# A decoder layer on one core: when x by tokens is loaded, where one block of x by features stands among the first weights, and which queue reloads the decay products

## The chip, the core and the metric

The kernel runs on one core of a Trainium2 chip. The core has TensorE (PE, matmuls), VectorE (DVE), ScalarE (ACT) and GpSimd (POOL) for arithmetic, and SyncE (SP), which here only issues transfers. SP, ACT and POOL each issue transfers from their own instruction stream, in order; a transfer that must wait for something holds up everything behind it on that engine. All transfers share 16 DMA engines. The metric is device time in microseconds (us) of one execution, lower is better.

## What is computed

One decoder layer, float32, 256 tokens by 2048 features, batch 1. Cut to the order of its parts:

```
def reference(x, mem, ...):
    x = x + 0.5 * swiglu(rms_norm(x, ffn1_norm), ffn1_w_gate, ffn1_w_up, ffn1_w_down)   # d_ff 5632
    x = gated_parallel_mixer(x, ...)      # p = rms_norm(x) @ w_in; sliding-window attention beside
                                          # RWKV-7 time mixing; gated sum @ w_out
    x = memory_cross_attention(x, mem, ...)
    x = x + 0.5 * swiglu(rms_norm(x, ffn2_norm), ffn2_w_gate, ffn2_w_up, ffn2_w_down)
    return rms_norm(x, final_norm)

def swiglu(h, w_gate, w_up, w_down):
    return (silu(h @ w_gate) * (h @ w_up)) @ w_down
```

RWKV-7 is a recurrence over time with a removal term. The kernel computes it in chunks of 128 tokens, which needs the inverse of a triangular matrix of products of decayed keys for each head and chunk. Those are the "decay products" of the change.

## The kernel before

**Weights.** All weights are read from DRAM once, in an order written out in `weight_plan` (L105) and cut into items of two 128-row blocks (L260 to L268). `load` (L275) issues an item's transfer on SP; in the feed-forward stages one unpaired load brings two items (1 MB, `wide`, L290), and a paired item (gate and up, or two column blocks of down) takes two transfers of 512 KB (L285). In the feed-forward stages there are three buffers of 1 MB (`raw2`, `RAW = 3`); in the mixer, four of 512 KB. A load waits on SP until its buffer is free.

**Products.** For precision every float32 operand is split in two: `hi`, its value cast to the matmul's format on ACT (L308), and `lo`, the rest, by a subtraction on DVE (L309). A product is three matmuls, hi by hi, lo by hi and hi by lo (`times`, L393: L396, L397, L398). `product` (L374) goes through the items of a column block; `next_item` (L356) issues loads ahead, splits the item and up to two items more, and returns the parts. `product_pair` (L454) is the paired form, in which some items take seven block products in place of eight: for these, `sums` (L321) makes differences of raw weights on DVE (L328 to L330) and splits them (L333, L334).

**Background work.** Everything else (norms, attention, the recurrence) is written as generators, which `Interleave` (L60) steps once in each tick; `product` ticks after each token half of an item, `product_pair` some 29 times in a column block. `idle(n)` (L175) lets n ticks pass. This sets the order in which the instructions are written down. From it the framework fixes the order on each engine when the program is built; on the chip an engine runs its instructions in that order, each as soon as what it needs is there. An instruction that waits for nothing runs as soon as its engine comes to it, however late its tick.

**The start (L762 to L790).** x by features (`xT`, for the matmuls' stationary side) is loaded in four blocks of 512 KB into `turned[0..3]`, the first in two halves, interleaved by hand on SP with the first loads of the gate weights:

```
first half of block 0, load 0 (one piece on ACT, two on SP), second half of block 0,
load 2 (two halves), block 1, load 4, block 2, load 6, block 3, load 8
```

`Norm.features` (L636) scales a block on ACT (`xhi`, L642) and takes the rest on DVE (`xlo`, L643); `squares` (L653) squares it on ACT (L655) and adds it up on DVE (L658, L662) for 1/rms, which reaches the first silu (L717) by PE (L667), DVE (L679) and POOL (L681). x by tokens, to which the results of the feed-forward are added, is loaded by `residual` (L785): four blocks of 512 KB over POOL's queue, 24 ticks apart. Its first reader is the end of the first down product (L570).

**The decay products (L1026 to L1114).** `removal_keys` computes them on PE and DVE and stores them over POOL to `ld` in DRAM (L1088), four times. `substitute` (L1093) reloads the diagonal blocks of 32 x 32 as `dl` with four transfers on SP (L1098), runs of 128 bytes, then waits 14 ticks and does the forward substitution in 62 small steps on DVE (L1105, L1110).

## Time and profile before

| | us |
|---|---|
| median of 3 runs (2276.04 to 2277.23) | 2276.31 |
| the profiled execution | 2275.04 |
| its span, first to last instruction | 2273.3 |
| PE busy in the span | 2248.3 |
| DVE busy | 1742.7 |
| ACT busy | 1213.6 |
| POOL busy | 128.9 |

The mean granted clock of PE over the span was 0.998. The DMA engines moved 434.63 MB, 191 GB/s on average.

How the views are read. A row of a timeline has start, duration, engine, line, operation, and written tile <- read tiles; the square brackets give the idle time ahead of it and what ended it. A row of the windows has the stretch, its length, then busy time and number of instructions of PE, PEld (weight loads of PE), DVE, ACT and POOL, the granted PE clock (1.00 is full), the mean busy share of the DMA engines and GB/s. A row of waits has who waited, for what, the sum, how many times, and the longest. A row of DMA issues has the tiles, the queue (SPq, POOLq), the number of transfers, KB each and the median us from issue to landing. The matmuls' durations overlap, since they are pipelined; in a full stretch one starts every 0.2275 us or so.

### The profile page before, as it was taken

Reading aid. Unit: us, or ns where it says so; the run is one execution under the profiler, and the core shown is the slowest. Engines: PE = TensorE matmul, PEld = TensorE weight load, DVE = VectorE, ACT = ScalarE, POOL = GpSimd, SP = SyncE. Lnnn points to the kernel's source line nnn. Section 1 sums busy time; section 2 is a strip of 40 time slices with the busy share of each in tenths; the row PEclk is TensorE's granted clock in tenths of the full one; section 3 lists DMA queues with packets and bytes.
Section 4 is the critical chain, followed back from the end, with each engine's and each line's share of the span. In section 5 each row is a group of like instructions: output and inputs, shape, how many; then the busy total and the mean of one; then the engine's idle time right before and its main releaser. Section 6 shows DMA issues by size and latency. Waiting matters only on the chain.

```text
span 2273.3 us, 28304 instructions
## 1 busy us (share of the span) xinstructions
PE 2248.3 (99%) x10588; PEld 1842.6 (81%) x10588; DVE 1742.7 (77%) x2120; ACT 1213.6 (53%) x1611; POOL 128.9 (6%) x184
## 2 busy tenths in 40 slices
PE   8999999999999999999999999999999999999998
PEld 6888888888888777788888888888888887888886
DVE  6988988889887567795444566547898888898887
ACT  6555555555555576444344546456555455555554
POOL 1000000000000001101220020001000000000002
PEclk9999999999999999999999999999999999999999
DMA  7665665666566545766432576557655665566664
GB/s 261 203 201 188 204 204 189 200 198 197 198 200 202 151 138 158 222 214 203 117 107 88 163 265 231 192 165 256 203 192 189 209 199 193 188 200 204 199 201 156
DMA packets 222890, 434.63 MB, mean 191 GB/s; under 512 B 17840, under 2 KB 19968, under 8 KB 222752
## 3 DMA queue, kind: packets, MB, share of 16 engines
q1 hardware_dynamic: 213840, 404.80, 55.8%
q0 software_dynamic: 8336, 27.22, 3.7%
q8 instruction: 83, 1.36, 0.2%
q10 hardware_dynamic: 576, 0.79, 0.1%
q14 instruction: 55, 0.45, 0.1%
HBM read 419.65 MB, written 13.11 MB: 190 GB/s over the span
## 4 chain that ended last, share of the span: by engine, by line
PE 93%; DVE 3%; DMA 2%; issue 1%; ACT 1%; POOL 0%; SPq 0%; POOLq 0%; ACTq 0%; DVEq 0%
PE acc L396 19%; PE acc L397 19%; PE acc L398 19%; PE mm L397 8%; PE mm L398 8%; PE mm L396 8%; PE tr L593 2%; PE tr L397 2%; PE tr L398 1%; PE tr L396 1%; PE mm L1247 1%; DVE lo L309 1%; PE tr L1216 1%; DMA raw<-in_ffn_w_gate_dram 1%; DMA raw<-in_ffn_w_up_dram 1%
## 5 line engine op out<-in xcount | busy, mean ns | idle before, releaser
L308 ACT CAST hi<-raw 128x1024 fp32r<-128x1024 f32 (+1 forms) x770 | 763.7, 1000 | 792.8 <-PE acc L398 393.9
L309 DVE TENSOR_TENSOR lo<-raw,hi 128x1024 fp32r<-128x1024 f32 (+1 forms) x770 | 891.2, 1168 | 373.7 <-ACT hi L308 372.5
L396 PE MATMUL acc<-hi,xhi 128*128 128x512 f32 (+1 forms) x1196 | 476.8, 399 | 7.7 <-ACT xhi L642 4.6
L397 PE MATMUL acc<-lo,xhi 128*128 128x512 f32 (+1 forms) x1196 | 466.0, 390 | 2.0 <-DVE lo L309 2.0
L398 PE MATMUL acc<-hi,xlo 128*128 128x512 f32 (+1 forms) x1196 | 464.9, 389 | 0.0
L396 PEld LDWEIGHTS acc<-hi,xhi 128*128 128x128 f32 x1196 | 224.9, 188 | 58.0 <-ACT xhi L642 5.5
L397 PEld LDWEIGHTS acc<-lo,xhi 128*128 128x128 f32 x1196 | 225.4, 188 | 48.2 <-DVE lo L309 3.2
L398 PEld LDWEIGHTS acc<-hi,xlo 128*128 128x128 f32 x1196 | 225.0, 188 | 47.0 <-issue 0.6
L333 ACT CAST thi<-raw 128x1024 fp32r<-128x1024 f32 x160 | 166.0, 1052 | 73.9 <-DVE raw L328 36.5
L334 DVE TENSOR_TENSOR tlo<-raw,thi 128x1024 fp32r<-128x1024 f32 x160 | 192.8, 1218 | 1.3 <-ACT thi L333 1.3
L397 PE MATMUL acc<-lo,hhi 128*128 128x512 f32 x404 | 158.0, 391 | 0.0
L398 PE MATMUL acc<-hi,hlo 128*128 128x512 f32 x404 | 157.8, 391 | 0.0
L396 PE MATMUL acc<-hi,hhi 128*128 128x512 f32 x404 | 157.3, 392 | 0.0
L396 PE MATMUL mm<-hi,xhi 128*128 128x512 f32 x380 | 149.1, 392 | 0.0
L397 PE MATMUL mm<-lo,xhi 128*128 128x512 f32 x380 | 148.3, 390 | 0.0
L398 PE MATMUL mm<-hi,xlo 128*128 128x512 f32 x380 | 148.1, 390 | 0.0
L328 DVE TENSOR_TENSOR raw<-raw 128x1024 f32<-128x1024 f32 x80 | 97.5, 1219 | 24.4 <-DMA raw<-in_ffn_w_up_dram 22.6
L397 PEld LDWEIGHTS acc<-lo,hhi 128*128 128x128 f32 x404 | 75.9, 188 | 17.4 <-DVE lo L309 2.3
L396 PEld LDWEIGHTS acc<-hi,hhi 128*128 128x128 f32 x404 | 75.9, 188 | 16.1 <-DVE x L551 0.9
L398 PEld LDWEIGHTS acc<-hi,hlo 128*128 128x128 f32 x404 | 75.9, 188 | 15.4
L397 PEld LDWEIGHTS mm<-lo,xhi 128*128 128x128 f32 x380 | 71.4, 188 | 15.6 <-DVE lo L309 0.6
L398 PEld LDWEIGHTS mm<-hi,xlo 128*128 128x128 f32 x380 | 71.3, 188 | 14.7
(374 smaller groups left out, 3407.4 us busy)
## 6 DMA issues: line engine op xcount, KB each, us to landing
raw<-in_ffn_w_gate_dram SPq DMA_DIRECT2D x167, 512.0 KB, 3.8
raw<-in_ffn_w_up_dram SPq DMA_DIRECT2D x160, 512.0 KB, 4.7
raw<-in_ffn_w_down_dram SPq DMA_DIRECT2D x152, 512.0 KB, 4.8
raw<-in_w_in_dram SPq DMA_DIRECT2D x136, 512.0 KB, 3.7
raw<-in_w_out_dram SPq DMA_DIRECT2D x32, 512.0 KB, 4.6
raw<-in_ffn_w_down_dram SPq DMA_DIRECT2D x12, 1024.0 KB, 5.2
raw<-in_ffn_w_up_dram SPq DMA_DIRECT2D x8, 1024.0 KB, 7.0
raw<-in_w_proj_attn_dram SPq DMA_DIRECT2D x16, 512.0 KB, 3.7
```

The lines of the kernel that those rows point to most:

```text
L308: newest["act"] = act.copy(hi[:, s], raw[:, s])
L309: newest["dve"] = dve.tensor_tensor(lo[:, s], raw[:, s], f32(hi[:, s]), ALU.subtract)
L328: dve.tensor_tensor(ta[:], raw[:, 1:3], raw[:, 0:2], ALU.subtract)
L333: act.copy(hi[:, s], t[:])
L334: dve.tensor_tensor(lo[:, s], t[:], f32(hi[:, s]), ALU.subtract)
L396: pe.matmul(o, xh, hi, start=first, stop=False, **how)
L397: pe.matmul(o, xh, lo, start=False, stop=False, **how)
L398: pe.matmul(o, xl, hi, start=False, stop=last, **how)
L593: pe.transpose(b[:, o : o + P], tok[:, t, col : col + P], ident[:])
L1216: pe.matmul(b[e][:, m * P : (m + 1) * P], x1[r, j, cs_], x2[r, j, cs_], start=True, stop=True,)
L1247: pe.matmul(vb[:, o : o + P][:, r], lhs(e), rhs[:, r], start=first and e == 0, stop=True, **ek,)
```

## The change

Three edits.

1. x by tokens is no longer loaded over POOL. `residual` waits 40 ticks, then 20 ahead of each block, and issues the block on SP, ordered behind the newest paired weight load (`newest["load"]`, which `load` now notes).
2. Among the first loads, block 1 of x by features goes ahead of the second half of load 2 (a piece of `load` may now be a call, `j is None`); blocks 2 and 3 then stand on both sides of load 4; loads 6 and 8 are left to `next_item`. The order on SP becomes: first half of block 0, load 0, second half of block 0, first half of load 2, block 1, second half of load 2, block 2, load 4, block 3, load 6, load 8.
3. The four reloads of the decay products are issued by POOL and not by SP.

```diff
@@ in load @@
             for v, c, to in zip(w, c0, (raw[:, 0:4:3], raw[:, 1:3])):
-                nc.sync.dma_start(
+                newest["load"] = nc.sync.dma_start(
                     to, v[rows, c : c + 512].rearrange("(a p) n -> p a n", p=P)
                 )
...
         for j, queue in pieces or ((slice(0, m * KU), nc.sync),):
+            if j is None:
+                queue()
+                continue
@@ the start @@
-        load(2, ((slice(0, 2), nc.sync), (slice(2, 4), nc.sync)))
-        for n in range(1, 4):
+        load(2, (
+            (slice(0, 2), nc.sync),
+            (None, lambda: nc.sync.dma_start(turned[1], a["xT"][:, 4:8])),
+            (slice(2, 4), nc.sync),
+        ))
+        for n in range(2, 4):
             nc.sync.dma_start(turned[n], a["xT"][:, 4 * n : 4 * n + 4])
-            load(2 * n + 2)
+            if n < 3:
+                load(2 * n)
...
         def residual():
+            yield from idle(40)
             for n in range(4):
-                yield from idle(24)
-                pool.dma_start(col(n), blk(W["x"], n))
+                yield from idle(20)
+                with tc.issue_after(newest["load"].ins):
+                    nc.sync.dma_start(col(n), blk(W["x"], n))
@@ in substitute @@
-                nc.sync.dma_start(dl[q], ld[q, :, q].rearrange("t h s -> h t s"))
+                pool.dma_start(dl[q], ld[q, :, q].rearrange("t h s -> h t s"))
```

## The prediction, made before the changed kernel was seen

> **What bounds the kernel now.** First the page: the busy line and the shares of the chain that ended last.

> ```profile
> PE 2248.3 (99%) x10588; PEld 1842.6 (81%) x10588; DVE 1742.7 (77%) x2120; ACT 1213.6 (53%) x1611; POOL 128.9 (6%) x184
> ...
> PE 93%; DVE 3%; DMA 2%; issue 1%; ACT 1%; POOL 0%; SPq 0%; POOLq 0%; ACTq 0%; DVEq 0%
> ```

> TensorE (PE) is busy for 2248.3 of 2273.3 us. The change removes no matmul, so all it can win is inside the other 25.0 us, or in stretches where PE is busy at a lower clock. Next I cut the span into windows of 20 us and looked for those where PE is not busy throughout. The six largest (columns: length, then busy us and count of PE, PEld, DVE, ACT, POOL; clock; DMA share; GB/s):

> ```profile
> 0.00:20.00 20.00, 14.80 (x67) 12.14 (x68) 9.89 (x18) 11.02 (x17) 8.59 (x34) 1.00 0.91 312
> 20.00:40.00 20.00, 17.11 (x70) 13.19 (x68) 15.00 (x20) 13.74 (x18) 1.48 (x1) 0.91 0.89 310
> 40.00:60.00 20.00, 19.13 (x84) 15.88 (x85) 15.69 (x25) 11.66 (x14) 0.09 (x1) 1.00 0.52 167
> 960.00:980.00 20.00, 18.15 (x80) 14.70 (x80) 17.80 (x44) 7.38 (x7) 0.72 (x1) 1.00 0.69 231
> 1900.00:1920.00 20.00, 18.28 (x81) 14.79 (x80) 18.11 (x21) 11.43 (x14) 0.00 (x0) 1.00 0.61 190
> 2260.00:2273.30 13.30, 4.97 (x22) 3.77 (x21) 4.30 (x10) 4.12 (x8) 1.13 (x2) 0.76 0.42 158
> ```

> The start loses 5.20 + 2.89 + 0.87 = 8.96 us, the end 8.33, and one window in the middle, 960 to 980, loses 1.85. The change touches the start (loads of x and of the first weights) and the reload of the decay products, which lies just before 960. It touches nothing at 1900 or at the end. So I read those two places.

> The start, by the stretches between PE's stops, and PE's first instruction after each stop:

> ```profile
> 12.84:15.31 2.47, 0.00 (x0) 0.00 (x0) 1.24 (x2) 1.09 (x3) 0.00 (x0) 1.00 1.03 392
> 15.31:20.87 5.56, 5.56 (x24) 4.43 (x24) 3.05 (x7) 2.21 (x4) 0.00 (x0) 1.00 1.04 389
> 20.87:23.19 2.32, 0.18 (x1) 0.00 (x1) 0.59 (x1) 1.60 (x3) 0.00 (x0) 1.00 1.02 389
> 23.19:28.60 5.41, 5.22 (x15) 3.89 (x16) 5.41 (x8) 5.17 (x9) 0.00 (x0) 0.68 1.05 391
> ```
> ```profile
> 15.31 0.50 PE L396 MATMUL acc<-hi,xhi 128*128 128x512 f32 x1 [2.47 <-ACT xhi L642]
> ...
> 23.19 0.50 PE L396 MATMUL acc<-hi,xhi 128*128 128x512 f32 x1 [2.14 <-ACT xhi L642]
> 23.88 0.50 PE L397 MATMUL acc<-lo,xhi 128*128 128x512 f32 x1 [0.18 <-DVE lo L309]
> ...
> 40.87 0.50 PE L396 MATMUL acc<-hi,xhi 128*128 128x512 f32 x1 [1.43 <-ACT hb L717]
> ```

> The DMA engines are full (share 1.02 to 1.05, 389 to 392 GB/s) while PE waits. What ScalarE (ACT) was waiting for:

> ```profile
> 9.73 1.05 ACT L308 CAST hi<-raw 128x1024 fp32r<-128x1024 f32 x1 [0.46 <-DMA raw<-in_ffn_w_gate_dram]
> ...
> 12.32 1.05 ACT L308 CAST hi<-raw 128x1024 fp32r<-128x1024 f32 x1 [0.58 <-DMA raw<-in_ffn_w_gate_dram]
> 14.75 1.71 ACT L642 ACTIVATE xhi<-xt,g_first 128x256 fp32r<-128x256 f32 x4 [1.38 <-DMA xt<-in_xT_dram]
> ...
> 21.52 1.04 ACT L308 CAST hi<-raw 128x1024 fp32r<-128x1024 f32 x1 [3.45 <-DMA raw<-in_ffn_w_gate_dram]
> ```

> Both large stops end with a transfer: the second block of x by features (14.75) and the third load of weights (21.52). Who fills the DMA engines is in the list of issues:

> ```profile
> x<-in_x_dram POOLq DMA_DIRECT2D x4, 512.0 KB, 10.5
> ...
> xt<-in_xT_dram SPq DMA_DIRECT2D x3, 512.0 KB, 16.5
> ```
> ```profile
> L788 POOL DMA_DIRECT2D x<-in_x_dram x4: 712/727/733, 6.5 to 8.6; - x4
> L570 DVE TENSOR_TENSOR x<-hb,x x4: 1216/1218/1218, 221.9 to 262.2; 128x1024 f32<-128x1024 f32 x4
> ```

> x by tokens (4 x 512 KB, 2.10 MB) is issued at 6.5 to 8.6 us, since GpSimd (POOL) has nothing to wait for and `idle(24)` delays only its place in the program. Its first reader runs at 221.9. It takes 2.10 MB / 390 GB/s = 5.4 us of a DMA system that PE is waiting for.

> **The change, part by part.** *x by tokens.* On SyncE's queue (SP) it sits behind paired weight loads that wait for free buffers, so it leaves the start. From about 9 to 21 us the weight queue then has the whole rate. The first half of load 2 lands at 9.73, as now; from there one 512 KB piece takes 524 KB / 390 = 1.35 us. In the new order: second block of x at 11.1, second half of load 2 at 12.4, third block of x at 13.8, load 4 (1 MB) at 16.5, fourth block at 17.8, load 6 at 20.5. Before, the second block came at 14.75 and load 4 at 21.52.

> *The block ahead of half a weight.* If the four scalings `xhi` go as the block lands, ACT does them in 11.1 to 12.8 (1.71 us, the row at 14.75), and PE, done with its first 24 matmuls at 12.84, goes on at once; the second half lands at 12.4, is cast after them (1.05) by 13.9, its rest is needed at 12.84 + 2.73 = 15.57 (12 matmuls, half of the 24 that would take 24 x 0.2275 = 5.46; the stretch of 5.56 shows it). If ACT keeps the old order (cast first), the scalings start at 12.4 + 1.05 = 13.45 and PE at about 13.9, 1.1 late. ACT's order is fixed when the program is built and follows readiness as the framework supposes it; a block ahead in the queue speaks for the first, which I take. Load 4 at 16.5 gives its cast by 17.6 and its rest by 18.8; PE needs them at 18.3 (cast) and 18.5 (rest). So stops of 2.47, 2.32 and 0.18 go. So does the low clock behind the second: 5.41 us at 0.68 lose 5.41 x 0.32 = 1.73 us. Sum: 6.70.

> What is late next is VectorE (DVE), whose work for a block of x and its two weight pieces is

> ```profile
> 15.29 1.69 DVE L643 SCALAR_TENSOR_TENSOR xlo<-xt,g_first,xhi 128x256 fp32r<-128x256 f32 x4 [0.67 <-ACT xhi L642]
> ...
> 18.11 1.23 DVE L658 TENSOR_TENSOR xt<-xt 128x1024 f32<-128x1024 f32 x1 [0.97 <-ACT xt L655]
> ```

> 1.69 + 1.23 + two rests of 1.22 (the `lo` row below) = 5.36 us against PE's 5.46. No cushion, so I give back 0.5 in small waits (bounds 0 and 1.1, the old order above). The wait of 1.43 at 40.87 ends with a chain of squares and 1/rms; PE arrives 6.7 us sooner, the DVE part of the chain perhaps not as much: another 0.5 (bounds 0 and 1.5). Start: 6.70 - 1.0 = 5.7 us won.

> *x behind the weights, between 90 and 170 us.* The program place is 60, 80, 100 and 120 ticks; a paired column block is about 29 ticks, the first two products about 36. Each issue costs SP under half a microsecond, each transfer 1.35 us behind a load, so it can make only the next load late. The closest the trace shows there:

> ```profile
> 70.00:170.00 100.00, 100.00 (x446) 81.92 (x445) 90.64 (x105) 57.45 (x64) 0.00 (x0) 1.00 0.60 196
> ```
> ```profile
> 92.80 1.23 DVE L328 TENSOR_TENSOR raw<-raw 128x1024 f32<-128x1024 f32 x1 [2.49 <-DMA raw<-in_ffn_w_up_dram]
> ...
> 100.90 1.23 DVE L334 TENSOR_TENSOR tlo<-raw,thi 128x1024 fp32r<-128x1024 f32 x1
> ```
> ```profile
> 104.91 0.39 PE L396 MATMUL tr<-thi,chi 128*128 128x512 f32 x1
> ```

> Even where DVE sat 2.49 us for a late load, the last difference made from it was done at 102.13 and PE read it at 104.91: 2.8 us of cover over 1.35. DMA is at 0.60 there. I cost it at 0; with the cover gone it is up to 4 x 1.35 = 5.4.

> *Decay products over GpSimd.* Now SP holds this (waits of SP's queue, then its issues):

> ```profile
> SPq L1098 <- DMA ld<-lt: 4.0, 1, 4.0
> ```
> ```profile
> 947.85 0.37 SPq L300 DMA_DIRECT2D raw<-in_w_in_dram  x1
> 952.43 2.70 SPq L1098 DMA_DIRECT2D dl<-ld  x4
> 955.23 11.92 SPq L300 DMA_DIRECT2D raw<-in_w_in_dram  x5
> ```
> ```profile
> 960.03 1.05 ACT L308 CAST hi<-raw 128x1024 fp32r<-128x1024 f32 x1 [2.59 <-DMA raw<-in_w_in_dram]
> ```
> ```profile
> 962.44 0.15 DVE L1105 TENSOR_TENSOR tmp<-xt,dl 128x1 f32<-128x1 f32 x1
> ...
> 965.54 1.22 DVE L309 TENSOR_TENSOR lo<-raw,hi 128x1024 fp32r<-128x1024 f32 x1
> ```
> ```profile
> 966.81 0.50 PE L397 MATMUL acc<-lo,xhi 128*128 128x512 f32 x1 [1.85 <-DVE lo L309]
> ```

> SP waits 4.0 us for the products to land in DRAM, issues four reloads in 2.70, and only then the next weight, at 955.23. That weight is cast at 960.03, and its `lo` stands in DVE's order behind some 3 us of substitution steps (962.44 on): PE loses 1.85. Over POOL, the wait holds POOL instead. Behind it there are

> ```profile
> 946.49 0.97 POOL L1100 MEMSET xt<- 128x1024 f32 x1
> ...
> 962.82 0.72 POOL L1131 DMA_DIRECT2D md<-ga  x1 [15.14 <-DVE xt L1110]
> ```

> a fill of 0.97 us (and a short one) and a store at 962.82. Four issues of about 0.72 (the store's row) from 952.4 end at 955.3, the fills by 956.5, the reload lands some 4 us after its issue, 959.5; DVE's first step at 962.44 has 3 us to spare. SP can issue the weight as its buffer frees, some 4 us sooner, and `lo` no longer falls behind those steps: 1.85 won (bounds 0, if DVE's order stays, and 1.85).

> **Sum.** 5.7 + 1.85 = 7.55 us. The profiled execution took 2275.04 (span 2273.3 and 1.7 around it): 2267.5. The median of the runs, 2276.31, lies 1.27 above it: 2268.8.

> **The rivals.** *The reload wins nothing:* DVE's fixed order still puts `lo` behind the steps. For it: the wait is set by that order; against it: the weight was truly 2.59 us late. 2270.6.

> *The low clock stays.* The stop of 2.47 us was followed by a clock of 1.00, the one of 2.32 by 0.68, so the length of the stop alone doesn't decide it, and a stop left over may bring it too. Then 1.73 is not won: 2270.5. [...]

> *The start is bound by DVE and ACT.* Old cast order (1.1 left in place of the 0.5), the 1.5 in the 1/rms chain in place of 0.5, and the low clock with them: 7.55 - 0.6 - 1.0 - 1.73 = 4.2 won, 2272.1.

> *The x transfers don't leave the start's critical path*, or what replaces them costs the same: 2276.3. Against it: the full DMA rows.

> *Slower: x on the weight queue starves the paired blocks.* If all four blocks catch a load without cover, each stop is like the largest for a late difference (1900 to 1920 loses 1.72), with a low clock of 1.73 behind it: 4 x 3.45 = 13.8 lost, 7.55 won, 2282.6. It decides from 7.55 / 4 = 1.9 us a block. Against it: 2.8 us of cover at the worst place seen.

> **How the numbers follow.** Forecast 0.56; reload wins nothing 0.12; clock stays 0.10; start bound by DVE and ACT 0.10; nothing gained 0.05; slower 0.07. A measurement of this kernel tells about 0.2%, 4.6 us, from no change, so faster is below 2271.8. Faster: 0.56 + 0.12 + 0.10 = 0.78, less 0.04 for two rivals coming together: 0.74. Same 0.18, slower 0.08. The lower end takes nothing back of the 6.70 (8.55 won, 2267.8) and leaves 1.3 for shifts in fixed orders elsewhere: 2266.5. The upper end takes in the start bound by DVE and ACT with the same 1.3: 2273.4.

> **What would show it.** Right: no stop of PE over 1 us between 7 and 36 us, clock 1.00 there, DMA of the start done some 5 us sooner; four x issues by SP between 80 and 170 without a stop of PE; no SP wait before the reload, PE whole from 960 to 980. Wrong: ACT casting the second half of load 2 ahead of the scalings; a longer wait at the 1/rms chain; a stop behind an x issue.

## The result, and the profile after

| | before | after |
|---|---|---|
| median of 6 runs each, us | 2275.97 (2273.84 to 2277.23) | 2267.45 (2265.83 to 2270.05) |
| ratio | | 0.9965, 95% interval 0.9952 to 0.9978 |
| the profiled execution, span | 2275.04, 2273.3 | 2266.59, 2264.9 |

The forecast was 2268.8; 8.5 us were won where 7.55 had been worked out. New code moves the lines: L308, L309 are L311, L312 after; L396 to L398 are L399 to L401; L642, L655, L717, L720 are L645, L658, L720, L723; L1098, L1105 are L1108, L1115.

The page of the changed kernel, busy line and shares of the chain:

```profile
PE 2248.1 (99%) x10588; PEld 1843.7 (81%) x10588; DVE 1742.6 (77%) x2120; ACT 1212.8 (54%) x1611; POOL 129.4 (6%) x184
...
PE 92%; DVE 3%; DMA 2%; issue 1%; ACT 1%; SPq 0%; POOLq 0%; POOL 0%; ACTq 0%; DVEq 0%
```

PE is busy for as long as before (2248.3); the idle time fell from 25.0 to 16.8 us. The windows say where (columns as before: length, busy us and count of PE, PEld, DVE, ACT, POOL, clock, DMA share, GB/s):

```profile
0.00:20.00 20.00, 17.99 (x70) 14.92 (x70) 12.03 (x23) 14.25 (x24) 5.83 (x30) 1.00 0.92 319
20.00:40.00 20.00, 19.08 (x87) 15.61 (x88) 14.92 (x22) 13.40 (x18) 1.80 (x1) 1.00 0.62 211
40.00:60.00 20.00, 20.00 (x90) 16.10 (x89) 19.06 (x27) 11.42 (x14) 0.00 (x0) 1.00 0.65 211
960.00:980.00 20.00, 20.00 (x90) 16.57 (x89) 19.00 (x43) 9.26 (x10) 0.00 (x0) 1.00 0.64 200
1900.00:1920.00 20.00, 18.59 (x82) 15.01 (x81) 16.40 (x19) 10.18 (x12) 0.00 (x0) 1.00 0.59 192
```

The first three lose 2.01 + 0.92 + 0 = 2.93 us (8.96 before), 960 to 980 loses nothing (1.85). The DMA share in 20 to 40 fell from 0.89 to 0.62: the first weights are no longer held up by x by tokens and land sooner (load 4 at 17.48 and not at 21.44). PE's stops in the start, in PE's timeline after:

```profile
6.94 1.22 PE L399 MATMUL acc<-hi,xhi 128*128 128x512 f32 x2 [0.82 <-ACT hi L311]
...
20.08 0.73 PE L399 MATMUL acc<-hi,xhi 128*128 128x512 f32 x2 [0.21 <-ACT hi L311]
...
21.66 0.50 PE L400 MATMUL acc<-lo,xhi 128*128 128x512 f32 x1 [0.84 <-DVE lo L312]
```

The stops of 2.47 and 2.32 are gone, and so is that of 1.43 behind 1/rms. What is left stands near 20 us. ACT's timeline says why:

```profile
10.61 1.05 ACT L311 CAST hi<-raw 128x1024 fp32r<-128x1024 f32 x1 [1.18 <-DMA raw<-in_ffn_w_gate_dram]
11.56 1.06 ACT L658 ACTIVATE xt<-xt 128x1024 f32<-128x1024 f32 x1
12.53 1.29 ACT L645 ACTIVATE xhi<-xt,g_first 128x256 fp32r<-128x256 f32 x3
13.72 1.04 ACT L311 CAST hi<-raw 128x1024 fp32r<-128x1024 f32 x1
14.66 2.10 ACT L645 ACTIVATE xhi<-xt,g_first 128x256 fp32r<-128x256 f32 x5
16.67 1.04 ACT L658 ACTIVATE xt<-xt 128x1024 f32<-128x1024 f32 x1
18.03 1.06 ACT L658 ACTIVATE xt<-xt 128x1024 f32<-128x1024 f32 x1 [0.31 <-DVE xlo L646]
19.00 1.98 ACT L311 CAST hi<-raw 128x1024 fp32r<-128x1024 f32 x2
```

Three of block 1's four scalings (12.53) now go ahead of the cast of the second half of load 2 (13.72). From 10.61 on ACT waits for nothing but 0.31 us. Load 4 landed at 17.48, but its cast comes at 19.00, when ACT gets to it: the squares of blocks 1 and 2 (16.67, 18.03) stand ahead. Before, this cast waited 3.45 us for its load.

The reload, in the timelines of SP, POOL and DVE after:

```profile
940.92 19.41 SPq L303 DMA_DIRECT2D raw<-in_w_in_dram  x8
...
946.06 3.17 POOL L1108 DMA_DIRECT2D dl<-ld  x4 [6.49 <-DMA ld<-lt]
...
955.99 1.23 DVE L312 TENSOR_TENSOR lo<-raw,hi 128x1024 fp32r<-128x1024 f32 x1 [0.30 <-ACT hi L311]
957.13 0.15 DVE L1115 TENSOR_TENSOR tmp<-xt,dl 128x1 f32<-128x1 f32 x1
```

SP issues its eight weights in one row; POOL holds the wait; on DVE `lo` stands ahead of the first substitution step. The issues of transfers (tiles, queue, count, KB, median us from issue to landing), after:

```profile
x<-in_x_dram SPq DMA_DIRECT2D x4, 512.0 KB, 5.6
...
dl<-ld POOLq DMA_DIRECT2D x4, 128.0 KB, 7.2
```

The four x blocks were issued at 94.0, 122.9, 151.3 and 183.7, 0.47 us each. PE had no stop over 0.1 us between 60 and 600 in this profile.

### The profile page after: what moved, and what is told of

The parts are those of the page before. It is cut to its first block, busy times and chain, and to the rows that moved or that the text cites. A ratio compares the mean times of both kernels' runs of the same rounds, so it can differ in the third digit from the quotient of the medians.

```text
span 2264.9 us, 28302 instructions
## 1 busy us (share of the span) xinstructions
PE 2248.1 (99%) x10588; PEld 1843.7 (81%) x10588; DVE 1742.6 (77%) x2120; ACT 1212.8 (54%) x1611; POOL 129.4 (6%) x184
## 4 chain that ended last, share of the span: by engine, by line
PE 92%; DVE 3%; DMA 2%; issue 1%; ACT 1%; SPq 0%; POOLq 0%; POOL 0%; ACTq 0%; DVEq 0%
PE acc L399 19%; PE acc L400 19%; PE acc L401 19%; PE mm L400 8%; PE mm L401 8%; PE mm L399 8%; PE tr L596 2%; PE tr L400 2%; PE tr L401 2%; PE tr L399 1%; DVE lo L312 1%; PE mm L1257 1%; PE tr L1226 1%; DMA raw<-in_ffn_w_up_dram 1%; ACT hi L311 1%
## 5 line engine op out<-in xcount | busy, mean ns | idle before, releaser
L311 ACT CAST hi<-raw 128x1024 fp32r<-128x1024 f32 (+1 forms) x770 | 763.6, 1000 | 787.8 <-PE acc L401 394.5
L312 DVE TENSOR_TENSOR lo<-raw,hi 128x1024 fp32r<-128x1024 f32 (+1 forms) x770 | 891.2, 1168 | 370.5 <-ACT hi L311 369.2
L399 PE MATMUL acc<-hi,xhi 128*128 128x512 f32 (+1 forms) x1196 | 477.0, 400 | 1.3 <-ACT hi L311 1.0
L401 PE MATMUL acc<-hi,xlo 128*128 128x512 f32 (+1 forms) x1196 | 464.9, 389 | 0.0
L399 PEld LDWEIGHTS acc<-hi,xhi 128*128 128x128 f32 x1196 | 225.0, 188 | 51.3 <-issue 5.4
L401 PEld LDWEIGHTS acc<-hi,xlo 128*128 128x128 f32 x1196 | 225.0, 188 | 47.0 <-issue 0.6
L401 PE MATMUL acc<-hi,hlo 128*128 128x512 f32 x404 | 157.8, 391 | 0.0
L399 PE MATMUL acc<-hi,hhi 128*128 128x512 f32 x404 | 157.2, 392 | 0.0
L399 PE MATMUL mm<-hi,xhi 128*128 128x512 f32 x380 | 149.1, 392 | 0.0
L401 PE MATMUL mm<-hi,xlo 128*128 128x512 f32 x380 | 148.1, 390 | 0.0
L399 PEld LDWEIGHTS acc<-hi,hhi 128*128 128x128 f32 x404 | 75.9, 188 | 16.0 <-DVE x L554 0.9
L401 PEld LDWEIGHTS acc<-hi,hlo 128*128 128x128 f32 x404 | 75.9, 188 | 15.3
L401 PEld LDWEIGHTS mm<-hi,xlo 128*128 128x128 f32 x380 | 71.3, 188 | 14.7
## 6 DMA issues: line engine op xcount, KB each, us to landing
raw<-in_ffn_w_gate_dram SPq DMA_DIRECT2D x167, 512.0 KB, 3.8
raw<-in_ffn_w_up_dram SPq DMA_DIRECT2D x160, 512.0 KB, 4.7
raw<-in_ffn_w_down_dram SPq DMA_DIRECT2D x152, 512.0 KB, 4.8
raw<-in_w_in_dram SPq DMA_DIRECT2D x136, 512.0 KB, 3.7
raw<-in_w_out_dram SPq DMA_DIRECT2D x32, 512.0 KB, 4.5
raw<-in_w_proj_attn_dram SPq DMA_DIRECT2D x16, 512.0 KB, 3.8
```

The source lines that it names most:

```text
L311: newest["act"] = act.copy(hi[:, s], raw[:, s])
L312: newest["dve"] = dve.tensor_tensor(lo[:, s], raw[:, s], f32(hi[:, s]), ALU.subtract)
L399: pe.matmul(o, xh, hi, start=first, stop=False, **how)
L401: pe.matmul(o, xl, hi, start=False, stop=last, **how)
```

## The experiments

**Theory A** is that of the prediction: the start is won by taking x out of the full DMA system and by moving the block; the reload wins 1.85 by DVE's order; x behind the weights costs nothing. The rivals: one edit does it all, the transfers only change places, the x blocks lack cover, or the clock makes the difference.

### One edit at a time

Edit 1 alone (x over SP behind the paired loads; the rest as before). Shown is `residual`; `load` notes `newest["load"]` as in the change:

```diff
+            yield from idle(40)
             for n in range(4):
-                yield from idle(24)
-                pool.dma_start(col(n), blk(W["x"], n))
+                yield from idle(20)
+                with tc.issue_after(newest["load"].ins):
+                    nc.sync.dma_start(col(n), blk(W["x"], n))
```

> The kernel before with the first edit alone: x by tokens behind the weights on SP, nothing else. Theory A (the x transfers took the rate that the start's weights and x by features needed): load 4 lands near 15 us instead of 21.5, the stop of PE of 2.3 us at 20.9 is gone, the one of 2.47 us at 12.8 shrinks to about 0.5 to 1.1 because ACT still casts the second half of load 2 ahead of the scalings; some 5 us won, ratio 0.9978. Theory B (the place of the block of x by features among the weights is what counts): the stop at 12.8 stays near 2 us, under 2 us won, ratio above 0.9990. The stop near 965 us (1.85) stays under both.

Edit 2 alone (block 1 ahead of the second half of load 2, blocks 2 and 3 on both sides of load 4; the rest as before). Not shown are `load`'s handling of the call and the loop behind, which are those of the change:

```diff
-        load(2, ((slice(0, 2), nc.sync), (slice(2, 4), nc.sync)))
+        load(2, (
+            (slice(0, 2), nc.sync),
+            (None, lambda: nc.sync.dma_start(turned[1], a["xT"][:, 4:8])),
+            (slice(2, 4), nc.sync),
+        ))
```

> The kernel before with the second edit alone: the block of x by features ahead of the second half of load 2, x by tokens still over POOL at the start. Theory A: the x transfers still take half the rate, block 2 stands ahead of load 4, so load 4 lands later, 22 to 23 us; the stop at 12.8 shrinks below 1 us, the stop for load 4 grows to 4 us or more; nothing won, ratio 0.9995 to 1.0010. Theory B: both stops shrink, 4 us or more won, ratio below 0.9983.

Edit 3 alone:

```diff
-                nc.sync.dma_start(dl[q], ld[q, :, q].rearrange("t h s -> h t s"))
+                pool.dma_start(dl[q], ld[q, :, q].rearrange("t h s -> h t s"))
```

> The kernel before with the third edit alone: the four reloads of the decay products on POOL. Theory: SP no longer waits 4 us ahead of the next weight, PE is whole from 960 to 980, 1.85 us won and no more, ratio 0.9992; the start is as before. Rival (the order on DVE keeps the rest of the weight behind the substitution): the stop of 1.85 us stays, ratio 1.0000.

Edits 1 and 2 together, the reload left on SP:

> The first two edits without the third. Theory A: the start of the changed kernel (about 6 us won), the stop of about 1.85 us near 960 us kept; ratio 0.9973, and the three parts add up to the change. If the second edit does nothing once x has left the start: the same as the first edit alone, within 0.5 us in the stops of PE before 40 us.

All four stood beside the same runs of the kernel before, median 2274.55 (25 runs):

| | median us (runs) | ratio | 95% interval | gain, us |
|---|---|---|---|---|
| edit 1 | 2268.67 (8) | 0.9976 | 0.9965 to 0.9986 | 5.9 |
| edit 2 | 2272.72 (11) | 0.9991 | 0.9983 to 1.0 | 1.8 |
| edit 3 | 2271.90 (11) | 0.9990 | 0.9981 to 0.9999 | 2.7 |
| edits 1 and 2 | 2267.67 (6) | 0.9971 | 0.9959 to 0.9982 | 6.9 |

Edit 1, edit 3 and edits 1 and 2 together have the ratios that theory A gave, within 0.0002. Edit 2 lies below its range (0.9991 where 0.9995 to 1.0010 was expected): it won a little where nothing was expected. The stop of 1.85 at the reload stays with edits 1, 2 and both, and is gone with edit 3. Edits 1 and 2 with 3 add up to 9.6, the whole change won 8.5. PE's stops between 12 and 60 us with edit 1 alone:

```profile
14.52 0.50 PE L396 MATMUL acc<-hi,xhi 128*128 128x512 f32 x1 [1.54 <-ACT xhi L642]
...
35.99 0.50 PE L396 MATMUL acc<-hi,xhi 128*128 128x512 f32 x1 [1.46 <-ACT hb L717]
```

The stop at 23 is gone, the first is shorter (1.54, where 0.5 to 1.1 was expected), the 1/rms stop has stayed. With edit 2 alone:

```profile
16.38 0.49 PE L399 MATMUL acc<-hi,xhi 128*128 128x512 f32 x1 [0.85 <-ACT hi L311]
17.64 0.52 PE L400 MATMUL acc<-lo,xhi 128*128 128x512 f32 x1 [0.77 <-DVE lo L312]
23.42 0.73 PE L399 MATMUL acc<-hi,xhi 128*128 128x512 f32 x2 [1.40 <-ACT hi L311]
24.68 0.69 PE L400 MATMUL acc<-lo,xhi 128*128 128x512 f32 x1 [0.53 <-DVE lo L312]
```

The stop behind block 1 has become stops behind weights, which x by tokens still holds up (load 4 landed at 22.25); the one for load 4 is 1.40 and 0.53 and not 4 or more, as was expected. The one at 1/rms is gone. So edit 1 makes the loads punctual, and edit 2 trades the wait for block 1 for one on weights and takes 1/rms off PE's path. With edit 3 alone the window at the reload is whole:

```profile
960.00:980.00 20.00, 20.00 (x90) 16.55 (x89) 18.09 (x44) 7.46 (x8) 0.89 (x2) 1.00 0.72 243
```

### x over POOL, but late

The kernel before, with x still on POOL's queue, but each issue ordered behind the first 1/rms, which runs on POOL (where `newest["rs"]` is noted is not shown):

```diff
+            while n1.r is None:
+                yield
             for n in range(4):
-                yield from idle(24)
-                pool.dma_start(col(n), blk(W["x"], n))
+                yield from idle(5)
+                with tc.issue_after(newest["rs"].ins):
+                    pool.dma_start(col(n), blk(W["x"], n))
```

> The kernel before, x by tokens still over POOL, but issued behind the first 1/rms on POOL, near 40 us, and not at 6.5 us. Nothing else is changed. Theory A (what counts is when the x transfers run, not on which queue): the start as in the first edit alone: load 4 lands near 17 us, no stop of PE at 20.9, the first silu's factors multiplied near 56.6 us and not 61.5; ratio 0.9978 within 0.0010. Rival (POOL's queue itself costs): less than half of that, ratio above 0.9989.

2272.89 (11 runs) against 2276.26 (21): 0.9988, interval 0.9979 to 0.9996. That is just between the two theories, and 2.5 us less than edit 1 alone won, so the time decides nothing. The profile does for the start: PE's stops there are

```profile
6.80 0.73 PE L396 MATMUL acc<-hi,xhi 128*128 128x512 f32 x2 [1.69 <-ACT hi L308]
13.64 0.50 PE L396 MATMUL acc<-hi,xhi 128*128 128x512 f32 x1 [0.83 <-ACT xhi L642]
34.84 0.79 PE L396 MATMUL acc<-hi,xhi 128*128 128x512 f32 x1 [1.44 <-ACT hb L717]
```

and the four transfers, issued from 34.0, stop nothing (0.28 us at 56.88 is all that is left before 60). The stops of 2.47 and 2.32 depend on x being in the start, not on the queue that carries it. This profile has two stretches at half clock, from 35.44 and from 963.33; what they are is the question of the last experiment. DVE's first up product starts at 57.34; the expectation was 56.6 in place of 61.5.

### All four x blocks behind one load

The changed kernel with the 20 ticks taken out of the loop, so that the four issues stand together:

```diff
             yield from idle(40)
+            yield from idle(20)
             for n in range(4):
-                yield from idle(20)
                 with tc.issue_after(newest["load"].ins):
```

> The changed kernel with its four x blocks behind one paired load and not behind four: 5.4 us of transfers in one place, more than the 2.8 us of cover that the prediction read there. Theory (the cover hides one block at a time): a stop of PE of 1 to 2.6 us some 10 us after it, perhaps with a half-speed stretch behind it; 1 to 4 us slower than the changed kernel, ratio 0.9970 to 0.9983. Rival (three buffers hide all four): no stop between 80 and 130 us, the changed kernel's time.

2266.97 (5) against 2276.26 (21): 0.9962, interval 0.9949 to 0.9976, as the whole change. My expectation of a stop fell. The window of the burst:

```profile
90.00:110.00 20.00, 20.00 (x89) 16.30 (x88) 19.49 (x23) 12.12 (x14) 0.00 (x0) 1.00 0.95 328
```

The DMA share goes to 0.95 and PE stays whole. The two weight transfers behind the four blocks landed 8.62 and 9.55 us after their issue, where 3.8 and 4.7 is the median: 4.8 us late, and PE didn't stop. So the cover here is at least that, and not the 2.8 that I read at one place: there I had taken the slack of one late piece, while three buffers of 1 MB stand between the queue and PE.

### The reload left on SP, the substitution written down later

The kernel before; only the first multiplication of the substitution is ordered behind the newest piece of DVE's work on weights:

```diff
-                dve.tensor_tensor(
+                with tc.issue_after(newest["dve"].ins) if t == 1 else nullcontext():
+                    dve.tensor_tensor(
 ...
```

> The kernel before with one edit: the first substitution step stands on DVE behind the rest of the newest weight; the four reloads stay on SP, so SP still waits 4 us ahead of the next weight, and that weight is still cast late. Theory A (what costs 1.85 us is DVE's order, eight substitution steps ahead of the rest of a late weight): the stop near 965 us is gone or under 0.4 us, some 1.85 us won, ratio 0.9992. Theory B (the late weight itself costs, whatever the order): a stop over 1 us stays.

2273.27 (11) against 2276.26 (21): 0.9989, interval 0.9980 to 0.9998; edit 3 alone had 0.9990. PE is busy for 20.00 of the 20 us from 960. SP's wait is still there (who waited, for what, sum, times, longest):

```profile
SPq L1098 <- DMA ld<-lt: 3.7, 1, 3.7
```

and the weight behind it is still late, but the order on DVE is another:

```profile
957.71 1.05 ACT L308 CAST hi<-raw 128x1024 fp32r<-128x1024 f32 x1 [2.11 <-DMA raw<-in_w_in_dram]
...
960.61 2.35 DVE L309 TENSOR_TENSOR lo<-raw,hi 128x1024 fp32r<-128x1024 f32 x2
963.81 1.22 DVE L309 TENSOR_TENSOR lo<-raw,hi 128x1024 fp32r<-128x1024 f32 x1 [0.85 <-ACT hi L308]
...
970.38 0.15 DVE L1106 TENSOR_TENSOR tmp<-xt,dl 128x1 f32<-128x1 f32 x1
```

ACT waits 2.11 us for the weight and PE loses nothing by it. So the late weight was not what cost 1.85 us; the eight substitution steps ahead of `lo` were.

### More idle matmuls ahead of the first product, and the same kernels again

The changed kernel's first product started at half speed: between 7 and 10.5 us its matmuls are 0.43 us apart in place of 0.23, and the 22 idle matmul records ahead of them (11 in the program) took 5.06 us, against 4.11 in the profile of before. So one kernel keeps PE busy longer ahead of the product:

```diff
-    for _ in range(11):
+    for _ in range(15):
         pe.matmul(idle_bank[:, :P], ones[:], ones[:], start=True, stop=True)
```

> The changed kernel with 15 in place of 11 idle matmuls ahead of the first product, so that PE has less of a gap ahead of it. Theory (the half-speed matmuls from 7 to 10.5 us of the changed kernel come from the gap or the short run before them): no matmul spaced 0.43 us before 12 us, up to 1.6 us won over the changed kernel, ratio 0.9958. Rival (where the half-speed stretch falls is chance): the changed kernel's time within 0.5 us, or a half-speed stretch elsewhere.

2264.09 (5) against 2276.26 (21): 0.9949, interval 0.9937 to 0.9962, the best of all, 12.2 us below before. There is no stretch at half speed in its profile between the first product and the kernel's last 10 us; but that doesn't yet say that the idle matmuls did it. What the clock does in the same kernel from one execution to the next, and what 20 idle matmuls do (the same line of the code), stood next to each other in the last four runs; the first two are the kernel before, unchanged. Theory A in them is that whether a stop brings half speed depends on where it falls in free windows of the clock, so that the same stops bring it in one execution and not in the next.

> The kernel before, unchanged, profiled a second time. Question: are the stretches at half speed (128x512 matmuls 0.43 us apart in place of 0.23, six to eight in a row) a property of the kernel's stops, or of where a stop falls in a clock window that runs freely? [...] Rival (the clock follows the stop's length or place): half speed at 24.5 again, for 8 matmuls, and nowhere else, in both.

> As the run ahead of it: the kernel before, unchanged, a third profile. Theory A (free windows): another pattern of half-speed stretches with the same stops. Rival: one stretch, 8 matmuls from 24.5, as in the first profile.

> The changed kernel, unchanged, in the same call as the next one. Ratio to before 0.9965 plus or minus 0.0010. Theory A (free windows): the same stops (0.8 before the first product, 0.7 and 0.8 near 20 to 22), the slow start until 10.5 not necessarily there again, and single times that scatter by some 3 us, as a stretch of half speed costs about 1.6 us. Rival: half speed again from 7.0 to 10.5 and times that scatter by less than 1 us.

> The changed kernel with 20 idle matmuls ahead of the first product in place of 11 (15 gave 2264.09 in an earlier call). Theory A: they run until the first cast is there (near 6.9 us), the stop of 0.8 before the first product shrinks to 0.1 or so, the clock is up from the first product on in every run; no faster than with 15, since 15 had the clock up too: 2264.1 plus or minus 1.0, some 3 us below the changed kernel, with single times within 1.5 us. Rival (the gain with 15 was chance): the same as the changed kernel, 2267. If the idle matmuls run past 7.0 us, the first product is late by what they overhang: at most 0.3.

The changed kernel came out at 2265.61 (5 runs, 2263.32 to 2267.29), ratio 0.9957, interval 0.9943 to 0.9970, against 2274.04 (9); with 20 idle matmuls it was 2264.69 (2264.07 to 2265.34), 0.9955, interval 0.9943 to 0.9968. The five runs with 15 lie within 1.25 us of each other, the five with 20 within 1.27; the six and the five of the changed kernel within 4.2 and 4.0. So the times with the longer warm-up are steadier, in five runs each. That it is faster is not shown: side by side the medians are 0.9 us apart where some 3 were expected, well inside the scatter of the changed kernel. Nor does the start end sooner: DVE's first up product starts at 55.96 with 15 and at 55.33 with 20 idle matmuls, at 55.70 in the changed kernel's first profile. With 20 the idle matmuls overran: the first product started at 7.83 and not at 6.94, 0.9 late where at most 0.3 was expected.

The windows of the half-speed stretches. The first profile of the kernel before:

```profile
24.45:27.83 3.38, 3.38 (x9) 2.60 (x9) 3.38 (x6) 3.13 (x6) 0.00 (x0) 0.50 1.03 391
```

The second:

```profile
16.40:19.80 3.40, 3.40 (x10) 2.67 (x9) 2.43 (x6) 1.62 (x3) 0.00 (x0) 0.51 1.03 386
965.38:968.37 2.99, 2.99 (x9) 2.32 (x7) 2.41 (x6) 0.19 (x1) 0.00 (x0) 0.50 0.86 257
```

The third:

```profile
14.63:18.00 3.37, 3.37 (x15) 2.79 (x16) 2.40 (x7) 2.22 (x4) 0.00 (x0) 1.00 1.03 385
25.18:28.17 2.99, 2.99 (x8) 2.30 (x7) 2.99 (x5) 2.74 (x4) 0.00 (x0) 0.50 1.03 388
967.07:970.06 2.99, 2.99 (x9) 2.34 (x8) 2.17 (x6) 0.61 (x1) 0.00 (x0) 0.50 0.87 259
```

The windows of 3.4 us here have 9 or 10 matmuls at a clock of 0.50, and 14 or 15 at 1.00. Behind the first large stop the clock fell in the second profile (0.51 from 16.40 to 19.80) and not in the first and third (1.00 from 15.31 to 20.87 and from 14.63 to 18.00); behind the 1.85 at the reload it fell in the second and third and not in the first (0.91, 0.91 and 1.00 over 960 to 980). The kernel is the same. That is as theory A had it; the rival, one stretch at 24.45, fell. The changed kernel, first its first profile, then its second:

```profile
6.94:10.52 3.58, 3.58 (x9) 2.76 (x9) 3.27 (x6) 2.42 (x5) 0.00 (x0) 1.00 1.00 301
```
```profile
6.94:10.34 3.40, 3.40 (x14) 2.52 (x15) 3.27 (x6) 3.01 (x6) 0.00 (x0) 1.00 0.96 334
22.21:25.60 3.39, 3.39 (x10) 2.65 (x8) 2.75 (x6) 1.40 (x2) 0.00 (x0) 0.51 0.75 242
```

9 matmuls against 14 at the same place: a slow start in the one and none in the other, which has a slow stretch at 22.21 instead. The clock column shows 1.00 for the slow start; only the count of matmuls betrays it. The column is made from the trace's records of the granted clock: the first record starts at 10.64 in the changed kernel's first profile and at 3.99 in the first of before, and ahead of it the column reads 1.00. The durations of the idle matmuls tell more. Their 22 records took 5.06 us in the changed kernel's first profile, all ahead of 10.64, and 4.62 in its second; with 15 idle matmuls 30 records took 5.00, and with 20 idle matmuls 40 took 7.01, where at the pace of the 5.06 they would have taken 6.9 and 9.2. So the clock rose while they ran; if their pace doubles then, that was near 4.2 and 5.9 us (an estimate from these durations), in both before 11 idle matmuls at half speed would have ended (6.12). By this estimate the added idle matmuls raised the clock in neither profile; why those times are steadier is open.

## Why the prediction was right, and where it was not

**What bounds the kernel** was right: PE's busy time stayed (2248.1), all that was won was idle time, in the two places named.

**The sum of the start was right within a microsecond, its terms were not.** That their errors cancel is luck. I took the stops of one profile as the kernel's own. Over the profiles of the same code, and those of experiments that leave the start as it is before or after:

| | idle of PE, 0 to 60 us | DVE's first up product (L720, after L723) starts at | half speed behind stops, 0 to 1000 us |
|---|---|---|---|
| before, first | 8.96 | 61.50 | from 24.45, 8 matmuls |
| before, second | 6.62 | 60.39 | 16.40, 8; 965.38, 7 |
| before, third | 8.67 | 61.40 | 25.18, 7; 967.07, 7 |
| edit 3 alone (start of before) | 6.73 | 61.78 | 15.65, 8; 40.18, 6 |
| substitution later (start of before) | 6.75 | 60.52 | 17.12, 7 |
| after, first | 2.93 | 55.70 | none (slow start until 10.52) |
| after, second | 4.30 | 56.82 | 22.21, 8 |
| edits 1 and 2 (start of after) | 4.66 | 56.93 | 21.85, 6 |
| x in a burst (start of after) | 4.08 | 54.93 | none |

On average the first up product comes 61.12 - 56.10 = 5.0 us sooner; I had 5.7.

- *Stops of 2.47, 2.32 and 0.18:* gone, as worked out, by the mechanism named: x left the full DMA system (edit 1, and again with x late on POOL), ACT scales the block ahead of the cast. In the first profile of before the four blocks of x by tokens land at 14.91, 17.03, 19.15 and 21.26, between block 1 (14.73) and load 4 (21.44). But the sum of 4.97 holds 0.18 us in which PE was busy (the row from 20.87), and it was that of one profile: over the five with the start of before these stops add up to 3.9 on average.
- *Low clock, 1.73:* the term that was mis-sized. Eight matmuls at 0.43 in place of 0.2275 cost 1.6 us, much as I had it, but what goes with a stop is only a chance of it. The five profiles with the start of before have six such stretches in their first 45 us, the four with the start of after have two: 0.7 fewer in an execution, some 1.0 us. The rival that kept the low clock was half right. More was won at the reload, where before had it in two of three profiles and the changed kernel has no stop to bring it.
- *Late next, DVE, 0.5 given back:* it was mostly ACT, whose squares I had left out. Block 1 landed at 12.12 and not at 11.1 (at 11.96 in the second profile, where ACT waits for it). From there ACT runs almost without a break:

```profile
10.52:20.00 9.48, 9.34 (x41) 7.38 (x39) 7.85 (x15) 9.08 (x15) 0.00 (x0) 1.00 1.04 396
```

  ACT is busy for 9.08 of 9.48 us, and with two squares ahead of it the cast of load 4 comes at 19.00, where I had it done at 17.6. With the clock up at the start (second profile) PE loses 1.14 and 0.84 us there, 2.0 in place of 0.5; the 0.84 is a wait for DVE, which has the rest behind the same cast. With the slow start PE arrives later and waits only 0.21 and 0.84: the slow start cost little, since ACT set the time anyway. Over the four profiles with this start PE loses 1.75 there.
- *1/rms, 0.5 given back:* wrong in sign; the stop of 1.43 was won. In the first profiles, before and after:

```profile
40.12 1.26 ACT L717 ACTIVATE hb<-acc,rs 128x512 f32<-128x512 f32 x2 [1.27 <-POOL rs L681]
```
```profile
33.31 1.27 ACT L720 ACTIVATE hb<-acc,rs 128x512 f32<-128x512 f32 x2
```

  The chain from the last square to the silu is no shorter (32.02 to 40.12 before, 25.20 to 33.31 after), but its start came 6.8 us sooner and PE's products did not come as much sooner. Edit 2 does that: the stop is there with edit 1 alone and gone with edit 2 alone. Loads 6 and 8 no longer stand in the starting order: the last block lands at 18.76, where it landed at 21.74 with edit 1 alone, and ACT squares it at 25.20 and not at 27.58.

With these averages the sum of the start is 3.9 for the stops, plus 1.0 for the clock, plus 1.4 at 1/rms, less 1.75 at ACT: 4.6, beside the measured 5.0.

**x behind the weights at 0** was right, with more cover than worked out (the burst). The rival that was slower needed 1.9 us a block; none was paid. One profile, that with 20 idle matmuls, has a stop of 1.33 us at 111.32, behind a weight that was issued at 102.67, nine microseconds behind an x block; no other profile has it, and what held that weight up is open. It took 6.13 us from issue to landing, in place of 4.6 in the first profile of after.

**The reload, 1.85 won,** was right. Of the two reasons that I gave together, SP's earlier issue and `lo` ahead of the steps, the second is enough by itself. The reload took 7.2 us (median) and not some 4; its last part landed at 956.11 and the first step came at 957.13, so it had 1.0 us to spare and not 3. The chance of lower clock behind that stop, 5 in 7 (of all profiles that have it: the clock over 960 to 980 is 0.91 in five and 1.00 in two) times 1.4 us (seven matmuls), came on top: some 1.0 us that the sum didn't hold. So 5.0 + 1.85 + 1.0 = 7.9 us, beside 7.05 between the mean spans of these profiles (2272.3 before, 2265.25 after) and 8.5 and 8.4 between the medians of the two comparisons. The rest is within what single executions scatter.

**What would show it:** no stop over 1 us between 7 and 36 held in the first profile (0.84 at most) and not in the second (1.14 at 19.58), nor did the clock of 1.00 there (0.51 from 22.21 to 25.60 in the second). The last x issue came at 183.7, later than the 170 named, and stopped nothing. The other signs held.

## What to carry to other kernels

Take a transfer that nobody needs for 200 us out of a stretch in which the DMA engines are full, and look at what its queue waits for: here POOL, which waited for nothing, issued the four x blocks at 6.5 to 8.6 us, though their places in the program were 24 to 96 ticks in. A late load and the stop behind it need not be cause and effect (here ACT waited 2.11 us for a weight and PE lost nothing); look at what stands ahead of the waiting work on its own engine. Before a term is put down to one stop or one stretch of low clock, see a second profile of the same kernel: here PE's idle time in the first 60 us differed by 2.3 us (8.96 and 6.62) and the clock by a whole stretch.

## What the runs showed of the hardware that was not expected

```profile
24.85:28.26 3.41, 3.41 (x10) 2.63 (x9) 3.41 (x5) 3.11 (x6) 0.00 (x0) 0.50 1.03 389
966.93:970.34 3.41, 3.41 (x10) 2.66 (x9) 2.31 (x6) 0.90 (x1) 0.00 (x0) 0.50 0.88 262
```

They start 942.08 us apart, which is 276 times 3.4133. The changes in the first profile of before lie 20.48, 3.41 and 2239.14 us apart, 6, 1 and 656 times 3.4133, and the two of after 2249.38, 659 times. Continued backwards, this grid begins 0.58 us behind the start of the span in the first profile of before, 0.96 in the third and 0.40 in the first of after: where a stop falls in it differed from one execution to the next.

Counted by this grid, in the first profile of before from 11 us to the last 10 us, six steps have more than 0.9 us of idle PE: 1.39 and 1.08 (the first large stop, which a border divides), 2.32 (the second), 1.43 (1/rms), 1.58 (the reload) and 1.72 (at 1912). Only behind the 2.32 did the clock fall. The same stop brought it in one profile and not in another: the 1.85 at the reload in five of seven, the one at 1/rms with edit 3 alone (1.44, half speed from 40.18) and with x late on POOL (1.44, from 35.44) and not in the first profile of before (1.43). How much idle time it takes, and whether that alone decides, is not shown.

**The reload over POOL's queue landed later.** Runs of 128 bytes, 128 KB a transfer: 4.1 us median on SP's queue before, 7.2 on POOL's after. Over all profiles it is 3.8 to 4.1 in the eight with SP's queue and 4.3 to 7.2 in the six with POOL's. The DMA engines were full in both while it ran (share 1.00 from 950 to 960 before, 1.04 from 945 to 955 after), so their load alone is not the reason; what makes it differ so much from one profile with POOL's queue to the next is open.
